# A decoder layer on one core: the causal mask moved from VectorE's scores to GpSimd's selects on the sigmoids, and two reorderings in the feed-forward part

## The chip, the cores and the metric

The kernel runs on one core of one Trainium2 chip. A core has a matrix engine (PE, with its weight loads PEld), VectorE (DVE), ScalarE (ACT), GpSimd (POOL) and a sync engine (SP) whose queue issues most DMAs. Each engine takes its instructions in order. The metric is the device time of one execution in microseconds; the time before is the median of three runs.

## The reference, cut to what matters

One decoder layer over 2048 tokens of width 1024: a norm, an input projection, two mixing groups (a causal convolution of width 31, and eight heads of causal stick-breaking attention), an output projection, a residual, and a SwiGLU feed-forward network of width 2816 with a residual. The part that the mask belongs to:

```python
z = einsum("bhqd,bhkd->bhqk", qb, kh) * scale
mask = key_pos[None, :] < q_pos[:, None]        # a token does not read itself
log_beta = log_sigmoid(z)
log_1m_beta = where(mask, log_sigmoid(-z), 0.0)
between = cumsum(log_1m_beta, axis=3, reverse=True) - log_1m_beta
attn = where(mask, exp(log_beta + between), 0.0)
```

So each weight is sigmoid(z) times the product of 1 - sigmoid(z) over the later keys. A masked key must give a factor of 1 in the product and a weight of 0.

## The kernel before, in words

**Tiling.** Tokens go in four groups of 512 (`g`), each of four 128-token tiles. Float32 products are made of three matmuls over split operands (H and L). A list `PLAN` names the stages on PE (input projection, output projection, first parts of the feed-forward network), and beside them run three "sides" with due positions: the attention, the convolution's taps (on DVE) and `sums`, which prepares combined feed-forward weights (on POOL).

**Order of instructions.** The text of the kernel gives each instruction a priority, in the order in which it is traced; the framework's scheduler then picks, engine by engine, what its model holds ready, higher priority first. So instructions traced late can run early. `tc.keep_in_program_order` pins an instruction behind the one traced just before it on the same engine. The feed-forward matmuls and the function `dve` (VectorE work of the loop `five`) are pinned so.

**Attention.** For each group, head (8) and key block `c` (from the diagonal one down to 0), `scores(u, j)` treats four tiles of 128 queries. Two matmuls write scores to a PSUM bank `z` (two of them, L563 and L564). On the diagonal block the width is (j + 1) x 128, and DVE adds `msk`, -1e30 above the diagonal, to the last 128 columns (L566). ACT makes `om` = sigmoid(-z/8) (L569) and `A` = sigmoid(z/8) (L571). DVE scans `om` from the right into running products (L573), which also reads `z`, so that the bank is free only after it, except in the last four heads of the last group. POOL multiplies `A` by the products (L574) and copies one column on for the next key block (L568, L576). `values` transposes `A` on PE (L590), splits it into TH (ACT, L248) and TL (DVE, L249), and multiplies by V (L595, L596). There are 128 diagonal calls of `scores` and 192 others.

**Feed-forward, gate and up.** It is done by a scheme with seven products of half size (numbered 1 to 7), whose right-hand sides are `B[g][n]`. `operands` loads such a side in four pieces (SP, L816), splits it on ACT (L810) and subtracts on DVE (L811). The loop `five` starts with block 0: `first` is product 6, and `second` adds a stored piece to it on DVE (L1061) before product 7 accumulates onto the same bank. Before the loop, sides 6, 5, 7 and 3 of the first half are loaded, 3 into tiles that the last output projection has just read. Product 3 of a block comes after products 7 and 5 and the next block's 6.

**Feed-forward, down.** 154 slots, each one pair of fetched pieces (SP loads, ACT splits L1279 and L1281, subtractions on POOL L1280 and DVE L1282, in rings of four) and 12 matmuls (L763). Slots go by product n = 1, 2, 6, 7, 4, 5, 3, eleven each, for two halves. When a row of the output is complete (n = 5, and n = 3), jobs are listed: `squares` (an ACT sum of squares, and a product by the gain on POOL, L1292) and `finish` (two POOL instructions that make the scale, L1297 and L1299, two DVE sums of 128x512, L1302, and the store of the row on SP, L1303). One job is traced to a slot. The last three slots are traced row by row, and their rows finished at once.

Of the kernel before, what the change touches and what calls it, by code (L numbers as in the profile page):

```python
# [9 lines left out]
F32 = mybir.dt.float32  # L10
# [3 lines left out]
ALU = mybir.AluOpType  # L14
# [4 lines left out]
P = 128  # L19
# [9 lines left out]
G = 512  # L29
NG = S // G  # L30
TT = G // P
# [3 lines left out]
NEG = -1e30  # L35
# [103 lines left out]
def layer_kernel(ctx: ExitStack, tc: tile.TileContext, x, xT, g_pre_mix, w_in, conv_w, conv_b, ln_g, ln_b,  # L139
                 attn_g, w_out, g_post_mix, g_pre_ffn, w_gate, w_up, w_down, g_post_ffn, out):  # L140
    nc = tc.nc
# [120 lines left out]
    def to_col(rows, k, Hs, Ls, g, banks=bank):  # L262

        ps = banks("tps")
        for t in range(TT):
# [24 lines left out]
    ident = ev("ident")[:, 0:P]  # L290
    make_identity(nc, ident)
    nc.vector.tensor_copy(idr, ident)
    msk = cc.tile([P, P], F32, name="msk")
    nc.gpsimd.memset(msk, NEG)
    nc.gpsimd.affine_select(msk, msk, pattern=[[1, P]], compare_op=ALU.is_ge, fill=0.0, base=0,
                            channel_multiplier=-1)
    one = cc.tile([P, 1], F32, name="one")
    nc.gpsimd.memset(one, 1.0)

# [234 lines left out]
    def attn(g):  # L534
# [20 lines left out]
        def scores(u, j):  # L555
            hd_ = heads[u["h"]]
            diag = u["c"] == g
            w = (j + 1) * P if diag else G
            K = u["K"]
            z = pp.tile([P, G], F32, tag="z", name="z")  # L560
            late = g == NG - 1 and u["h"] >= NH // 2
            js = slice(j * P, (j + 1) * P)
            nc.tensor.matmul(z[:, 0:w], hd_["QL"][:, js], K[:, 0:w], start=True, stop=False)  # L563
            nc.tensor.matmul(z[:, 0:w], hd_["QH"][:, js], K[:, 0:w], start=False, stop=True)  # L564
            if diag:
                nc.vector.tensor_tensor(z[:, w - P:w], z[:, w - P:w], msk, ALU.add)  # L566
            om = ap.tile([P, G + 1], F32, tag="om", name="om", bufs=NOM)
            nc.gpsimd.tensor_copy(om[:, G:G + 1], hd_["prev"][j])  # L568
            nc.scalar.activation(om[:, G - w:G], z[:, 0:w], AF.Sigmoid, scale=-0.125)  # L569
            a = ap.tile([P, G], F32, tag="A", name="A", bufs=NA)  # L570
            nc.scalar.activation(a[:, 0:w], z[:, 0:w], AF.Sigmoid, scale=0.125)  # L571
            r = om[:, G - w:G + 1][:, ::-1]
            nc.vector.tensor_tensor_scan(r, r, (one if late else z[:, 0:1]).to_broadcast([P, w + 1]), one, ALU.mult, ALU.bypass)  # L573
            nc.gpsimd.tensor_tensor(a[:, 0:w], a[:, 0:w], om[:, G - w + 1:G + 1], ALU.mult)  # L574
            pv = sp.tile([P, 1], F32, tag="pv", name="pv", bufs=8)
            nc.gpsimd.tensor_copy(pv, om[:, G - w:G - w + 1])  # L576
            hd_["prev"][j] = pv
            u["A"].append(a)
            return w
# [56 lines left out]
        for n in range(len(units) + 1):  # L636
            u = None
            if n < len(units):
                h, c = units[n]
# [345 lines left out]
    with ExitStack() as E:  # L985
# [113 lines left out]
        def five(early, todo):  # L1099


            NB = len(blocks)

            class Block:
                def __init__(self, n):
                    self.n = n
                    self.g, self.i, self.j = blocks[n]
                    self.A = {}
                    self.ahead = weights(*blocks[n], self.A)
                    next(self.ahead)  # L1110
                    self.s1 = next(s1_)
                    self.c11 = self.A["c11"]
                    nc.sync.dma_start(self.s1, stored["c11", self.g, self.i, self.j, 0])
                    nc.sync.dma_start(self.c11, stored["c11", self.g, self.i, self.j, 1])

                def mul(self, ps, n, start):
                    product(ps, n, self.A, B[self.g], start)
                    flush(2)

                def first(self):  # L1120
                    self.b2 = gu("b2")
                    self.mul(self.b2, 6, True)

                def second(self):
                    self.u2 = next(u_)
                    dve(self.u2, self.b2, self.s1, add)

                def split(self):
                    if "L" in self.A:
                        self.A["L"]()  # L1130

            b = Block(0)
            for _ in b.ahead:
                pass
            b.split()
            b.first()
            b.second()
            behind = []
            more_h = []
            for n in range(NB):  # L1140
                b3 = gu("b3")
                b.mul(b.b2, 7, False)
                nxt = Block(n + 1) if n + 1 < NB else None
                for fn, *args in behind:
                    fn(*args)
                c11 = result(b.i, (1, 1), b.c11)
                b.mul(b3, 5, True)
                u3 = next(u_)
                dve(u3, b.b2, b.s1, add)
                p4_ = b.A.get("p4")  # L1150
                if p4_ is not None:
                    dve(p4_, u3, p4_, add)
                if more_h:
                    next(more_h.pop())
                dve(u3, b3, u3, add)
                if nxt:
                    next(nxt.ahead)
                    nxt.first()
# [12 lines left out]
                if p4_ is None:  # L1171
                    p4_ = b.b2
                    dve(p4_, p4_, b.s1, add)
                c21 = result(b.i, (2, 1), p4_)
                b.mul(b3, 3, False)
                c21()
                dve(b3, b3, b.u2, add)
                behind = [(result(b.i, (1, 2), b3),)]
                if b.i:
                    more_h.append(hidden(b.g, b.j))  # L1180
                    behind.append((next, more_h[0]))
                behind += todo.get(n, ())
                b = nxt
            for fn, *args in behind:
                fn(*args)
            next(more_h.pop())
            assert next(more, None) is None
            next(more_wd)
            for _ in range(12):
                flush(2)  # L1190

        operands(0, [(6, x2), (5, x2), (7, e[4:6]), (3, e[0:2])])
        R = []
        last = NG - 2

# [95 lines left out]
            nc.scalar.activation(junk, t, AF.Square, scale=D ** -0.5, accum_out=ss[g][:, c, q:q + 1])  # L1291
            eng.tensor_tensor(t, t, gm[:, c * G:(c + 1) * G], mult)  # L1292

        def finish(T, r, cs):
            ms = sp.tile([P, 1], F32, tag="msf", name="msf", bufs=4)
            g, q = T // (2 * TT), T % (2 * TT)
            nc.gpsimd.tensor_scalar(ms, ss[g][:, 0, q:q + 1], ss[g][:, 1, q:q + 1], EPS, add, add)  # L1297
            rs = sp.tile([P, 1], F32, tag="rs", name="rs", bufs=4)
            nc.gpsimd.tensor_tensor(rs, ms, nhalf[:, 0:1], ALU.pow)  # L1299
            for (c, t) in enumerate(cs):  # L1300
                cs_ = slice(c * G, (c + 1) * G)
                nc.vector.scalar_tensor_tensor(r[:, cs_], t, rs, r[:, cs_], mult, add)  # L1302
            nc.sync.dma_start(out[T * P:(T + 1) * P, :], r)  # L1303

        LASTJ = 3
        slots = [(g, n, j) for g in (0, NG - 2) for n in (1, 2, 6, 7, 4, 5, 3) for j in range(HF)]
# [14 lines left out]
        for i, (g, n, j) in enumerate(slots):  # L1321
# [12 lines left out]
            if j == HF - 1:  # L1334
                for t, ps in enumerate(pss):
# [5 lines left out]
                    elif n in (6, 7):  # L1341
                        nc.vector.tensor_tensor((u2s if n == 6 else u3s)[t], ps, s1s[t], add)
                    elif n == 4:
                        nc.vector.tensor_tensor(s1s[t], ps, s1s[t], add)
                        jobs.append((squares, TB + t, 0, s1s[t]))
                    elif n == 5:
                        nc.vector.tensor_tensor(u3s[t], ps, u3s[t], add)
                        jobs.append((squares, TB + t, 1, u3s[t]))
                        jobs.append((finish, TB + t, hrows[t], (s1s[t], u3s[t])))
                    else:  # L1350
                        if ending:
                            for m in range(LASTJ):
                                slot(i - LASTJ + 1 + m, t, ps)
                        nc.vector.tensor_tensor(u2s[t], ps, u2s[t], add)
                        if ending:
                            squares(TA + t, 1, u2s[t], nc.vector)
                            finish(TA + t, hrows[TT + t], (c11s[t], u2s[t]))
                        else:
                            jobs.append((squares, TA + t, 1, u2s[t]))
                            jobs.append((finish, TA + t, hrows[TT + t], (c11s[t], u2s[t])))  # L1360
            elif jobs:
                fn, *args = jobs.pop(0)
                fn(*args)
        assert not jobs
    C.close()

# [56 lines left out]
```

## Time and profile before

| | us |
|---|---|
| median of 3 runs | 2562.7 (2555.69 to 2565.44) |
| profiled execution, its own time | 2551.76 |
| its span, first to last instruction | 2549.9 |

The mean granted clock of PE in the profiled execution is 0.983. The profile gives, for each engine, busy time; for each group of like instructions (line, engine, tiles, shapes), count, busy time, mean duration in ns, and the idle time of the engine just before them with what ended it. A wait's row reads: engine, tile and line that waited, what ended the wait, total us, times, longest. A timeline row reads: start, duration, engine, line, operation, tiles, count, and in brackets the engine's idle time before it and what ended that. Where a wait is for several things the profile names the one that came last by its records.

The stages in the trace: attention and projections up to about 1500 us, the loop `five` from about 1523 to about 2120 us, `down` from there to the end.

### The profile page before, as it was taken

How to read it: one execution, taken by the hardware profiler on the slowest of the kernel's cores; microseconds unless marked ns; L12 is line 12 of the kernel's file. 1: busy time of each engine (PE TensorE's matmuls, PEld its weight loads, DVE VectorE, ACT ScalarE, POOL GpSimd, SP SyncE). 2: the span in 40 equal slices, each digit the busy share in tenths (PEclk: the TensorE clock that was granted, in tenths of full speed). 3: DMA queues.
4: the chain of work that ended last, by engine and by line, in shares of the span. 5: the costliest groups of instructions: out<-in, count | busy, mean ns of one | idle time of the engine just before them, and what ended most of it. 6: DMA issues, size and time to landing. Idle time of an engine off the chain costs nothing. (4 is left out here: it accounts for less than half of the span.)

```text
span 2549.9 us, 35685 instructions
## 1 busy us (share of the span) xinstructions
PE 2422.0 (95%) x11156; PEld 1956.1 (77%) x11156; DVE 1806.7 (71%) x2321; ACT 1291.8 (51%) x2398; POOL 1518.6 (60%) x1844
## 2 busy tenths in 40 slices
PE   7999989998999999999999979999999999998997
PEld 6878767776777778887788857777788888886886
DVE  5797689977998797886655547667666664556556
ACT  4555555655655655667766644333322324454443
POOL 5764678555643666449634428755656564567556
PEclk9999989998999999999999989999999999999999
DMA  9989977987586698747877747977878768668665
GB/s 348 324 294 321 289 253 272 379 281 243 199 288 199 217 332 305 264 145 248 306 227 236 236 138 283 321 252 242 311 272 276 264 235 279 192 194 284 199 190 173
DMA packets 289181, 657.31 MB, mean 258 GB/s; under 512 B 33888, under 2 KB 42080, under 8 KB 288992
## 3 DMA queue, kind: packets, MB, share of 16 engines
q1 hardware_dynamic: 264704, 622.01, 72.7%
q10 hardware_dynamic: 24288, 33.04, 3.7%
q8 instruction: 88, 1.44, 0.2%
q14 instruction: 101, 0.83, 0.1%
HBM read 460.92 MB, written 193.99 MB: 257 GB/s over the span
## 5 line engine op out<-in xcount | busy, mean ns | idle before, releaser
L574 POOL TENSOR_TENSOR A<-A,om 128x512 f32<-128x512 f32 (+2 forms) x320 | 327.4, 1024 | 357.5 <-DVE om L573 234.9
L1054 POOL TENSOR_TENSOR wL<-raw,wH 128x512 fp32r<-128x512 f32 x176 | 253.5, 1463 | 202.7 <-ACT wH L1053 196.9
L476 DVE SCALAR_TENSOR_TENSOR cv<-glu,cw,cv 128x512 f32<-128x512 f32 x464 | 346.8, 748 | 6.7
L573 DVE TENSOR_TENSOR_SCAN om<-om,one,z 128x513 f32<-128x513 f32 (+3 forms) x256 | 278.0, 1098 | 62.4 <-ACT A L571 48.6
L1282 DVE TENSOR_TENSOR xL__21961<-t__21963,xH__21960 128x512 fp32r<-128x512 f32 x154 | 196.7, 1286 | 158.7 <-ACT xH__21960 L1281 158.7
L1280 POOL TENSOR_TENSOR xL__21959<-t__21962,xH__21958 128x512 fp32r<-128x512 f32 x154 | 209.7, 1367 | 165.5 <-ACT xH__21958 L1279 160.9
L256 PE MATMUL inps<-xH,wL 128*128 128x512 f32 x640 | 259.5, 406 | 5.5 <-ACT sg L422 5.5
L260 PE MATMUL inps<-xL,wH 128*128 128x512 f32 x640 | 257.2, 403 | 0.0
L258 PE MATMUL inps<-xH,wH 128*128 128x512 f32 x640 | 257.1, 402 | 0.0
L249 DVE TENSOR_TENSOR TL<-at,TH 128x512 fp32r<-128x512 f32 (+1 forms) x320 | 188.4, 598 | 89.1 <-ACT TH L248 88.5
L569 ACT ACTIVATE om<-z 128x512 f32<-128x512 f32 (+2 forms) x320 | 171.3, 538 | 157.8 <-DVE z L566 67.5
L763 PE MATMUL dps<-xH__21958,xL__21961 128*128 128x512 f32 x616 | 241.1, 391 | 10.3 <-DVE xL__21961 L1282 8.9
L763 PE MATMUL dps<-xL__21959,xH__21960 128*128 128x512 f32 x616 | 240.6, 391 | 3.2 <-POOL xL__21959 L1280 3.2
L763 PE MATMUL dps<-xH__21958,xH__21960 128*128 128x512 f32 x616 | 240.5, 390 | 0.0
L248 ACT ACTIVATE TH<-at 128x512 fp32r<-128x512 f32 (+1 forms) x320 | 168.6, 546 | 98.2 <-PE at L590 84.5
L1279 ACT ACTIVATE xH__21958<-t__21962 128x512 fp32r<-128x512 f32 x154 | 97.1, 631 | 229.0 <-POOL xL__21959 L1280 142.3
L590 PE MATMUL at<-idr,A 128*128 128x128 f32 x1088 | 191.2, 279 | 6.0 <-POOL A L574 3.8
L210 ACT ACTIVATE wH<-raw 128x1024 fp32r<-128x1024 f32 x156 | 165.8, 1063 | 55.1 <-DMA raw<-in_w_in_dram 23.0
L1053 ACT ACTIVATE wH<-raw 128x512 fp32r<-128x512 f32 x176 | 101.1, 623 | 158.9 <-PE b L763 65.1
L590 PEld LDWEIGHTS at<-idr,A 128*128 128x128 f32 x1088 | 142.0, 144 | 42.2 <-POOL A L574 6.1
L571 ACT ACTIVATE A<-z 128x512 f32<-128x512 f32 (+2 forms) x320 | 168.1, 540 | 10.8 <-PE at L590 10.5
L847 POOL TENSOR_TENSOR sum<-sum 128x512 f32<-128x512 f32 x88 | 115.6, 1313 | 74.6 <-DMA sum<-in_w_up_dram 42.4
(301 smaller groups left out, 6380.3 us busy)
## 6 DMA issues: line engine op xcount, KB each, us to landing
wL<-wL SPq DMA_DIRECT2D x156, 512.0 KB, 4.7
raw<-in_w_in_dram SPq DMA_DIRECT2D x80, 512.0 KB, 5.9
t__21963<-u SPq DMA_DIRECT2D x154, 256.0 KB, 2.8
c<-c ACTq DMA_DIRECT2D x88, 256.0 KB, 4.5
t__21962<-wd SPq DMA_DIRECT2D x88, 256.0 KB, 3.0
K<-kd SPq DMA_DIRECT2D x80, 256.0 KB, 4.4
V<-vd SPq DMA_DIRECT2D x80, 256.0 KB, 3.9
u<-accf SPq DMA_DIRECT2D x22, 768.0 KB, 4.3
```

The source lines that it names most:

```text
L249: nc.vector.tensor_tensor(L, ps, H.bitcast(F32), ALU.subtract)
L256: nc.tensor.matmul(ps, WL[:, kc], aH[t](k), start=k == 0, stop=False)
L258: nc.tensor.matmul(ps, WH[:, kc], aH[t](k), start=False, stop=False)
L260: nc.tensor.matmul(ps, WH[:, kc], aL[t](k), start=False, stop=k == KT - 1)
L476: nc.vector.scalar_tensor_tensor(to, gl[c][:, k:k + G], cw[:, c, k:k + 1], a, ALU.mult, ALU.add))
L573: nc.vector.tensor_tensor_scan(r, r, (one if late else z[:, 0:1]).to_broadcast([P, w + 1]), one, ALU.mult, ALU.bypass)
L574: nc.gpsimd.tensor_tensor(a[:, 0:w], a[:, 0:w], om[:, G - w + 1:G + 1], ALU.mult)
L590: nc.tensor.transpose(pt[:, j * P:(j + 1) * P], u["A"][j][:, b * P:(b + 1) * P], id32)
L763: return nc.tensor.matmul(ps, a, b, skip_group_check=True, **flags)
L1054: nc.gpsimd.tensor_tensor(l, t, f32(h), sub)
L1280: nc.gpsimd.tensor_tensor(WL, w, f32(WH), sub)
L1282: nc.vector.tensor_tensor(UL, t, f32(UH), sub)
```

## The change

1. The mask tile and the DVE addition go. After both sigmoids of a diagonal call, POOL runs an affine select on the last 128 columns of each: 1.0 into `om` and 0.0 into `A` where the key is not before the query.
2. Side 3 of the first half is no longer loaded with sides 6, 5 and 7 ahead of the loop, but is traced after `first` and `second` of block 0.
3. In `down`, `finish` does one half of a row; the scale is made at the first half and kept for the second; the store is a job of its own (`put`). A slot takes one job, or two if the first is a store; in the last slots as many as are needed to empty the list.

```diff
-    msk = cc.tile([P, P], F32, name="msk")
-    nc.gpsimd.memset(msk, NEG)
-    nc.gpsimd.affine_select(msk, msk, pattern=[[1, P]], compare_op=ALU.is_ge, fill=0.0, base=0,
-                            channel_multiplier=-1)
...
-            if diag:
-                nc.vector.tensor_tensor(z[:, w - P:w], z[:, w - P:w], msk, ALU.add)
             om = ap.tile([P, G + 1], F32, tag="om", name="om", bufs=NOM)
             nc.gpsimd.tensor_copy(om[:, G:G + 1], hd_["prev"][j])
             nc.scalar.activation(om[:, G - w:G], z[:, 0:w], AF.Sigmoid, scale=-0.125)
             a = ap.tile([P, G], F32, tag="A", name="A", bufs=NA)
             nc.scalar.activation(a[:, 0:w], z[:, 0:w], AF.Sigmoid, scale=0.125)
+            if diag:
+                for t, x, fill in ((om, G, 1.0), (a, w, 0.0)):
+                    t = t[:, x - P:x]
+                    nc.gpsimd.affine_select(t, t, pattern=[[-1, P]], compare_op=ALU.is_ge, fill=fill, base=-1,
+                                            channel_multiplier=1)
...
             b.first()
             b.second()
+            operands(0, [(3, e[0:2])])
...
-        operands(0, [(6, x2), (5, x2), (7, e[4:6]), (3, e[0:2])])
+        operands(0, [(6, x2), (5, x2), (7, e[4:6])])
...
-        def finish(T, r, cs):
+        def scale_of(T, c):
+            if c:
+                return scales.pop(T)
             ms = sp.tile([P, 1], F32, tag="msf", name="msf", bufs=4)
             g, q = T // (2 * TT), T % (2 * TT)
             nc.gpsimd.tensor_scalar(ms, ss[g][:, 0, q:q + 1], ss[g][:, 1, q:q + 1], EPS, add, add)
             rs = sp.tile([P, 1], F32, tag="rs", name="rs", bufs=4)
             nc.gpsimd.tensor_tensor(rs, ms, nhalf[:, 0:1], ALU.pow)
-            for (c, t) in enumerate(cs):
-                cs_ = slice(c * G, (c + 1) * G)
-                nc.vector.scalar_tensor_tensor(r[:, cs_], t, rs, r[:, cs_], mult, add)
+            scales[T] = rs
+            return rs
+
+        def finish(T, r, t, c):
+            rs = scale_of(T, c)
+            cs_ = slice(c * G, (c + 1) * G)
+            nc.vector.scalar_tensor_tensor(r[:, cs_], t, rs, r[:, cs_], mult, add)
+
+        def put(T, r):
             nc.sync.dma_start(out[T * P:(T + 1) * P, :], r)
+
+        def rest(T, r, cs):
+            return [(finish, T, r, t, c) for c, t in enumerate(cs)] + [(put, T, r)]
...
-                        jobs.append((finish, TB + t, hrows[t], (s1s[t], u3s[t])))
+                        jobs += rest(TB + t, hrows[t], (s1s[t], u3s[t]))
...
             elif jobs:
-                fn, *args = jobs.pop(0)
-                fn(*args)
+                left = len(slots) - i - LASTJ
+                for _ in range(-(-len(jobs) // max(left, 1)) if left < HF else 2 if jobs[0][0] is put else 1):
+                    if jobs:
+                        fn, *args = jobs.pop(0)
+                        fn(*args)
```

More of the change, by code (lines that the diff above doesn't have):

```diff
@@ L1299, in finish @@
             nc.gpsimd.tensor_tensor(rs, ms, nhalf[:, 0:1], ALU.pow)
[L1300 to L1302 removed]
+            scales[T] = rs
+            return rs
+        scales = {}
+        def finish(T, r, t, c):
[3 more added lines that the diff above has]
+        def put(T, r):
             nc.sync.dma_start(out[T * P:(T + 1) * P, :], r)
+        def rest(T, r, cs):
+            return [(finish, T, r, t, c) for c, t in enumerate(cs)] + [(put, T, r)]
         LASTJ = 3
@@ L1356, in layer_kernel @@
                             squares(TA + t, 1, u2s[t], nc.vector)
-                            finish(TA + t, hrows[TT + t], (c11s[t], u2s[t]))
+                            for fn, *args in rest(TA + t, hrows[TT + t], (c11s[t], u2s[t])):
+                                fn(*args)
                         else:
                             jobs.append((squares, TA + t, 1, u2s[t]))
-                            jobs.append((finish, TA + t, hrows[TT + t], (c11s[t], u2s[t])))
+                            jobs += rest(TA + t, hrows[TT + t], (c11s[t], u2s[t]))
             elif jobs:
-                fn, *args = jobs.pop(0)
-                fn(*args)
+                left = len(slots) - i - LASTJ
+                for _ in range(-(-len(jobs) // max(left, 1)) if left < HF else 2 if jobs[0][0] is put else 1):
+                    if jobs:
+                        fn, *args = jobs.pop(0)
+                        fn(*args)
         assert not jobs
```

## The prediction

> **What bounds the kernel now.** I read the first part of the page, then the waits of TensorE (PE) by stage, then the timeline at each long one.
>
> ```profile
> span 2549.9 us, 35685 instructions
> PE 2422.0 (95%) x11156; PEld 1956.1 (77%) x11156; DVE 1806.7 (71%) x2321; ACT 1291.8 (51%) x2398; POOL 1518.6 (60%) x1844
> ...
> PE 27%; POOL 2%; DVE 2%; DMA 2%; issue 1%; ACT 0%; SPq 0%; POOLq 0%; DVEq 0%; ACTq 0%
> ```
>
> PE is busy 2422.0 of 2549.9 us and leads the chain that ended last. The change takes no matmul away, so what it can win is PE's idle time, 127.9 us (5%), and time in which PE runs at half pace behind a pause. I therefore price each edit by the PE waits that it touches. The mask lies in the attention stage, 64 to 1430 us:
>
> ```profile
> 64.00:1430.00 1366.00, 1302.87 (x6334) 1052.64 (x6333) 1071.07 (x1537) 818.88 (x1552) 806.03 (x1275) 0.98 0.80 267
> ...
> PE z L563 <- DVE om L573: 23.3, 31, 2.7
> PE o L596 <- DVE TL L249: 10.8, 16, 1.7
> ```
>
> The first row holds the busy time of PE, PEld, DVE, ACT, POOL in that window; the others are waits (us, times, longest). PE idles 1366 - 1302.87 = 63.1 us there, 23.3 of it for a score bank that the scan (DVE L573) has not let go. DVE is busy 78%, POOL 59%.
>
> **The change, part by part: the mask.** Removed from DVE: 128 additions. Added to POOL: 256 affine selects of 128x128, an instruction that this trace shows in its prologue.
>
> ```profile
> L566 DVE TENSOR_TENSOR z<-z,msk 128x128 f32<-128x128 f32 x128 | 36.7, 291 | 38.4 <-PE z L564 38.2
> ACT om L569 <- DVE z L566: 67.5, 41, 6.4
> 1.62 0.29 POOL L295 TENSOR_SCALAR_AFFINE_SELECT msk<-msk 128x128 f32<-128x128 f32 x1
> L563 PE MATMUL z<-K,QL 128*128 128x512 f32 x224 | 97.2, 434 | 15.3 <-DVE om L573 14.4 <-DMA vd<-vt 0.7
> ```
>
> - DVE loses 128 x 0.291 = 36.7 us of work, and 38.2 us in which it stood at an addition waiting for scores. ACT no longer waits 67.5 us (41 times) for the addition: 0.5 us for each of 128 diagonal units.
> - POOL gains 256 x 0.29 = 74.2 us, 5% of the stage: 59% becomes 64%. The memset and select of the mask (0.2 + 0.29 us) go from the prologue, where the engines wait for input DMAs: nothing.
> - Sigmoid, scan and product keep shapes and counts. But the scan, in DVE's in-order queue, now waits for the select of om, which stands in POOL's in-order queue behind whatever is there. Behind the scan are the taps and the TL subtractions, for which PE waits. The select of A sits before the product on the same engine: 0.29 us of POOL's idle time.
>
> On one side the gain is at most what the narrow diagonal scores wait for (the 512-wide ones wait 14.4 of 23.3 us, so the others 8.9) and the 10.8 us for TL: 19.7. On the other stands what a late select costs; the nearest rows are those in which POOL's head holds up a scan today:
>
> ```profile
> 605.89 1.26 POOL L847 TENSOR_TENSOR sum<-sum 128x512 f32<-128x512 f32 x1 [5.72 <-DMA sum<-in_w_up_dram]
> 607.31 1.28 DVE L573 TENSOR_TENSOR_SCAN om<-om,one,z 128x513 f32<-128x513 f32 x1 [3.44 <-POOL om L568]
> 608.65 0.50 PE L563 MATMUL z<-K,QL 128*128 128x512 f32 x1 [2.68 <-DVE om L573]
> POOL sum L847 <- DMA sum<-in_w_up_dram: 42.4, 12, 10.4
> POOL sum L847 <- DMA sum<-in_w_gate_dram: 20.0, 11, 7.9
> POOL wL L214 <- ACT wH L210: 31.4, 12, 4.9
> ```
>
> A sum waits 5.72 us for its DMA, the one-column copy behind it is late, the scan stalls 3.44 us and PE 2.68. Such foreign waits at POOL's head make 42.4 + 20.0 + 31.4 = 93.8 us, 7% of the stage. If 7% of 128 selects (9) meet one of 2.7 us (93.8 / 35), scans wait 24 us, PE 2.68/3.44 of it, 19 us. Mostly a select lands between products of 1.0 to 1.2 us, which costs as much as the 0.5 us saved. I take 7 us gained: the 8.9 us of the narrow banks largely, a little of TL, less a few late selects. Ends: 19.7 gained, 19 lost.
>
> The Trainium skill ("GPSIMD Engine Reference", section 4.1 Engine selection) would keep elementwise work on VectorE: GpSimd is about twice slower with two inputs and about line rate with one. The row bears out the exception, 0.29 us against VectorE's 0.291. Priced as two-input work at twice that, POOL would gain 149 us by estimate, and the late-select rival would weigh more.
>
> **P3's side.** Moving operand 3 behind `second` moves four loads on SP, four ACT splits and four DVE subtractions. `second` is pinned behind the DVE instruction traced before it: today the last of those subtractions.
>
> ```profile
> 1499.49 2.12 SPq L816 DMA_DIRECT2D sumin<-B  x4
> 1525.71 0.40 PE L763 MATMUL b<-xL__17306,wH 128*128 128x512 f32 x1
> 1524.87 4.66 DVE L811 TENSOR_TENSOR e__17360<-sumin,e__17359 128x512 fp32r<-128x512 f32 x4 [0.83 <-ACT e__17359 L810]
> 1529.45 0.68 DVE L1061 TENSOR_TENSOR glu<-b,glu 128x512 f32<-128x512 f32 x1
> 1530.28 0.47 PE L763 MATMUL b<-e__17341,wL 128*128 128x512 f32 x1 [4.17 <-POOL ms L191]
> 1531.38 0.63 PE L763 MATMUL b<-e__17341,wL 128*128 128x512 f32 x1
> 1531.81 0.63 PE L763 MATMUL b<-e__17341,wH 128*128 128x512 f32 x1
> 1534.23 0.39 PE L763 MATMUL b<-e__17341,wH 128*128 128x512 f32 x1
> 1534.46 0.39 PE L763 MATMUL b<-e__17342,wH 128*128 128x512 f32 x1
> ```
>
> The product ends at 1526.1; `second` (glu) runs only at 1529.45, behind the four subtractions of 1.165 us; PE restarts after 4.17 us. (The row names POOL's ms; glu ends 0.15 us before PE starts, and it is glu that must read the bank before PE adds to it.) Then eight matmuls run 0.43 us apart instead of 0.23: 8 x 0.2 = 1.6 us more. With `second` free of the pin, it waits for one running subtraction at most: 1526.1 + 1.17 + 0.68 + 0.15 = 1528.1, a wait of 2.0 instead of 4.17. Elsewhere PE paused 2.4 us and the next matmul took full pace (below, 2307.37), so the 1.6 go too: 3.8 us. Ends: nothing, if all four subtractions still run first as they are ready earlier; 4.17 - 0.8 + 1.6 = 5.0 if none does. The subtractions end some 0.7 us later; P3's product comes three products of 2.8 us (12 x 0.23) behind, which covers it. The four loads, issued on SP at 1499.49, come to stand behind the first block's weight loads; they have the 25 us up to the subtractions in hand. A later wait could give some back: 3 us taken.
>
> The Trainium skill ("TensorE: Matmul & The Clock Gate", Part 1) puts the array at half clock after an idle window of about 3.4 us. By it a wait left at 3.5 us would keep the slow 1.6 us, and the edit would be worth 0.7; the 4.17 and 2.37 us rows agree with it.
>
> **The row ends.** Work is the same; `finish` becomes two halves and a store, each a job of its own.
>
> ```profile
> 2292.30 1.15 POOL L1297 TENSOR_SCALAR msf<-ss 128x1 f32<-128x1 f32 x1
> 2293.53 1.30 POOL L1292 TENSOR_TENSOR e__21967<-e__21967,gain 128x512 f32<-128x512 f32 x1
> 2302.17 1.78 DVE L1302 SCALAR_TENSOR_TENSOR e__21969<-t__21965,rs,e__21969 128x512 f32<-128x512 f32 x1
> 2303.87 1.77 DVE L1302 SCALAR_TENSOR_TENSOR e__21969<-e__21967,rs,e__21969 128x512 f32<-128x512 f32 x1
> 2305.57 4.65 DVE L1282 TENSOR_TENSOR xL__21961<-t__21963,xH__21960 128x512 fp32r<-128x512 f32 x4
> 2296.95 0.50 PE L763 MATMUL dps<-xL__21959,xH__21960 128*128 128x512 f32 x1 [0.61 <-POOL xL__21959 L1280]
> 2307.37 0.50 PE L763 MATMUL dps<-xH__21958,xL__21961 128*128 128x512 f32 x1 [2.37 <-DVE xL__21961 L1282]
> 2333.50 0.50 PE L763 MATMUL dps<-xL__21959,xH__21960 128*128 128x512 f32 x1 [2.00 <-POOL xL__21959 L1280]
> 2343.92 0.50 PE L763 MATMUL dps<-xH__21958,xL__21961 128*128 128x512 f32 x1 [2.41 <-DVE xL__21961 L1282]
> 2518.49 0.50 PE L763 MATMUL dps<-xL__21959,xH__21960 128*128 128x512 f32 x1 [0.61 <-POOL xL__21959 L1280]
> 2528.89 0.50 PE L763 MATMUL dps<-xH__21958,xL__21961 128*128 128x512 f32 x1 [2.38 <-DVE xL__21961 L1282]
> ```
>
> At three row ends DVE runs final sums in a heap, up to 1.78 us each, and the operand subtractions (L1282) behind them keep PE waiting: 0.61 + 2.37, 2.00 + 2.41, 0.61 + 2.38, in all 10.4 us. Split jobs rank behind more operand work, so sums and subtractions should alternate. Against it: jobs stand one to a slot of 2.8 us (12 matmuls) already, yet row ends came in a burst; one row's msf (2292.30) and the next row's product by the gain (2293.53) stand 1.2 us apart, where their slots are two apart: the scheduler pulls ready work forward whatever its slot. At the last row end both versions use two slots a row. I take half of the first two, 7.4 us: 4, and nothing of the last. Ends: 7.4 gained; 3 lost, if a late store on SP holds a load behind it by a slot.
>
> **Sum.** 7 + 3 + 4 = 14 us. The profiled execution took 2551.76 us (span 2549.9): 2538 on its footing. It lies 10.9 us under the median of the runs, 2562.7; on that footing 2548.
>
> **Rivals.** Half a per cent, 12.8 us, is about what a measurement here tells from no change.
>
> - Likeliest: the sum, 2548; its own range 2536 to 2558.
> - Reordering eats it. The scheduler floats selects, splits and row ends to where they are ready; `second` still runs behind the subtractions, the row ends still heap, and the mask trades one queue for another at 0.5 us each. Left: about 4 us, 2559. For it: the burst above. Against: the pin on `second` does go.
> - Slower: selects stuck at POOL's head. 9 late selects lose 19 us of PE; each pause above 3 us adds half-paced matmuls, 1.6 us a time. With one select in eight late, 16 x 2.7 x 0.78 = 34 us, against 12 us still won (3 + 4, and 5 of the mask's): 22 lost, 2585. It decides from about 12 late ones (25 - 12 = 13 us). For it: the 605.89 row. Against: POOL has 41% idle, and its copies today cost scans only 6.3 us in sum:
>
> ```profile
> DVE om L573 <- POOL om L568: 6.3, 4, 3.4
> ```
>
> - More gain: with 75 us off DVE's queue (36.7 + 38.2), all 19.7 us of scan and TL waits, 5 and 7.4 go: 32 us, 2531.
>
> **Chances.** The sum 0.38, reordering 0.32, slower 0.16, more gain 0.14. Of the sum's outcomes some fall short of 12.8 us, so faster takes most of 0.38, and 0.14: 0.47; same 0.36; slower 0.17. The range 2524 to 2578 goes from just past the full gain to short of the stuck selects.
>
> **What would show it.** Mask: L566 gone, 256 selects near 0.29 us, "z waits for om" under 23.3 us; wrong if a wait of the scan for POOL's select appears above some 25 us. P3: glu starts before the last L811 subtraction and the 4.17 us pause is at or under 2; wrong if it stays. Row ends: waits for L1282 and L1280 at the first two under 4 us; wrong if final sums still stand in a row of six. The whole is wrong if PE's idle time does not fall, or the order of the attention stage changes for other reasons and moves it by more than 15 us.

## The result and the profile after

The changed kernel takes 2571.5 us (median), before takes 2555.9 in the same session: ratio 1.0055, 95% interval 1.004 to 1.007. It is 16 us slower where I forecast 14 us faster. Two executions of it were profiled, 2580.3 us (called "after" below) and 2573.1 ("second profile"); the second is near the median, so the stage readings are from it. Executions of one program spread over 10 to 14 us, so all verdicts below go by ratios over the runs with their 95% intervals, and a row of a trace is only read for its mechanism.

The head of after's page: PE's span share falls by a point, DVE loses 10 us (23 in the second profile), POOL gains 72.

```profile
span 2578.6 us, 35988 instructions
PE 2431.4 (94%) x11156; PEld 1962.4 (76%) x11156; DVE 1796.2 (70%) x2193; ACT 1292.6 (50%) x2398; POOL 1590.5 (62%) x2098
```

The attention stage, from 64 us to the first matmul of the last gate-and-up stage, by windows: before, then the second profile.

```profile
64.00:1523.00 1459.00, 1384.23 (x6693) 1116.57 (x6692) 1118.90 (x1597) 867.62 (x1639) 835.08 (x1316) 0.98 0.78 261
```

```profile
64.00:1542.00 1478.00, 1389.55 (x6704) 1119.26 (x6703) 1094.21 (x1469) 868.60 (x1640) 908.30 (x1573) 0.97 0.77 259
```

The stage is 19 us longer. PE idles 1478 - 1389.55 = 88.5 us in it instead of 74.8; the other 5.3 us are busy time, for 11 matmuls more (some 2 us) and at a granted clock of 0.97 instead of 0.98. The rest of the kernel is 2.5 us longer (2571.4 - 1542 against 2549.9 - 1523). So the loss lies in the stage of the mask; the first experiment shows that it is the mask's.

The selects, and the waits of the second profile (64 to 1560 us):

```profile
L570 POOL TENSOR_SCALAR_AFFINE_SELECT A<-A 128x128 f32<-128x128 f32 x128 | 40.6, 321 | 30.5 <-ACT A L565 29.6 <-DVE om L573 0.2
L570 POOL TENSOR_SCALAR_AFFINE_SELECT om<-om 128x128 f32<-128x128 f32 x128 | 40.6, 318 | 69.6 <-ACT om L563 64.2 <-PE z L560 3.8 <-DMA kd<-qkL 1.2
```

```profile
ACT om L563 <- PE z L560: 131.8, 99, 6.6
POOL om L570 <- ACT om L563: 64.2, 43, 4.2
DVE om L573 <- POOL om L570: 34.5, 26, 4.2
PE z L559 <- DVE om L573: 27.4, 31, 3.3
```

Before, ACT waited for the scores so long, beside the 67.5 us for the addition:

```profile
ACT om L569 <- PE z L564: 63.9, 50, 6.3
```

A select takes 0.32 us instead of the 0.29 priced: 81 us for 256. The scan (L573) waits 34.5 us, 26 times, for a select; before it waited 6.3 us for POOL's one-column copy and 13.1 us for POOL in all. POOL in turn stands idle ahead of selects for 100 us (69.6 + 30.5), nearly all of it until ACT has made the sigmoid. PE's wait for a score bank did not fall: 27.4 against 23.3. And ACT gained nothing by the addition's going: it waits 131.8 us for the scores now, where it waited 63.9 + 67.5 = 131.4 us for the scores and the addition.

**One place that shows it.** Around 135 us PE stops for 5.2 to 6.3 us in each profile of the changed kernel itself (four orders, below) and in no profile of before. Second profile, ACT and PE:

```profile
133.90 1.06 ACT L210 ACTIVATE wH<-raw 128x1024 fp32r<-128x1024 f32 x1 [4.33 <-DMA raw<-in_w_in_dram]
135.13 0.27 ACT L563 ACTIVATE om<-z 128x128 f32<-128x128 f32 x1
135.28 0.28 ACT L565 ACTIVATE A<-z 128x128 f32<-128x128 f32 x1
136.44 0.65 ACT L660 ACTIVATE oT<-o 128x512 f32<-128x512 f32 x1
137.14 0.80 PE L595 MATMUL o<-TH,V 128*128 128x512 f32 x1 [5.88 <-ACT oT L660]
```

The same place before:

```profile
130.59 1.06 ACT L210 ACTIVATE wH<-raw 128x1024 fp32r<-128x1024 f32 x1 [5.41 <-DMA raw<-in_w_in_dram]
131.55 0.58 ACT L660 ACTIVATE oT<-o 128x512 f32<-128x512 f32 x1
132.18 0.50 PE L595 MATMUL o<-TH,V 128*128 128x512 f32 x1 [1.13 <-ACT oT L660]
```

In both, ACT's queue stands behind a weight that a DMA brings. Before, the copy of `oT`, which frees PE's bank `o`, is next; in the changed kernel it comes after the sigmoids of two diagonal units, and the weight lands 3.3 us later. Nothing here is a late select: it is the other order that the scheduler draws once the work of a diagonal unit looks different to it. Why the weight landed later was not traced. Nor is this stop the whole loss: e6 and e11 below have selects and lose as much or more, and wait only 0.9 and 1.7 us for `oT` there.

**P3's side and the row ends, after.** DVE and PE at the first, DVE and PE at the second:

```profile
1554.29 4.06 DVE L811 TENSOR_TENSOR e__17775<-sumin,e__17774 128x512 fp32r<-128x512 f32 x3 [0.84 <-ACT e__17774 L810]
1558.27 0.68 DVE L1061 TENSOR_TENSOR glu<-b,glu 128x512 f32<-128x512 f32 x1
1559.09 0.47 PE L763 MATMUL b<-e__17722,wL 128*128 128x512 f32 x1 [3.57 <-POOL rs L192]
...
2329.50 0.74 DVE L1312 SCALAR_TENSOR_TENSOR e__22349<-e__22348,rs,e__22349 128x512 f32<-128x512 f32 x1
2330.82 1.78 DVE L1312 SCALAR_TENSOR_TENSOR e__22350<-e__22348,rs,e__22350 128x512 f32<-128x512 f32 x1
2335.93 4.64 DVE L1283 TENSOR_TENSOR xL__22342<-t__22344,xH__22341 128x512 fp32r<-128x512 f32 x4
2337.73 0.50 PE L763 MATMUL dps<-xH__22339,xL__22342 128*128 128x512 f32 x1 [2.44 <-DVE xL__22342 L1283]
2373.46 0.50 PE L763 MATMUL dps<-xH__22339,xL__22342 128*128 128x512 f32 x1 [2.41 <-DVE xL__22342 L1283]
```

Three of the four subtractions still run ahead of `second` (glu); the pause is 3.57 us instead of 4.17. The final sums (L1312) still stand six in a row (2327.80 to 2336.0, two of them shown), the subtractions behind them, and PE's waits are 2.44 and 2.41 where they were 2.37 and 2.41.

### The profile page after: what moved, and what is told of

The parts are those of the page before. It is cut to its first block, busy times and chain, and to the rows that moved or that the text cites. A ratio compares the mean times of both kernels' runs of the same rounds, so it can differ in the third digit from the quotient of the medians.

```text
span 2578.6 us, 35988 instructions
## 1 busy us (share of the span) xinstructions
PE 2431.4 (94%) x11156; PEld 1962.4 (76%) x11156; DVE 1796.2 (70%) x2193; ACT 1292.6 (50%) x2398; POOL 1590.5 (62%) x2098
## 5 line engine op out<-in xcount | busy, mean ns | idle before, releaser
L574 POOL TENSOR_TENSOR A<-A,om 128x512 f32<-128x512 f32 (+2 forms) x320 | 319.3, 999 | 251.6 <-DVE om L573 185.5
L573 DVE TENSOR_TENSOR_SCAN om<-om,one,z 128x513 f32<-128x513 f32 (+3 forms) x256 | 276.4, 1097 | 67.6 <-ACT A L565 45.0
```

## The experiments

"Before" and "after" are the two kernels, with the attention's due times ending at 870 (`ATTN = ((46, 0.0), (870, 1.0))`). Ratios are to before, from the same chip and session.

**The two other edits alone (e1).**

```diff
 # after, with before's mask back
+nc.vector.tensor_tensor(z[:, w - P:w], z[:, w - P:w], msk, ALU.add)
-nc.gpsimd.affine_select(t, t, ...)      # on om and on A
```

> The kernel before with P3's side fetched later and the row ends split, and the mask still added by VectorE. In the changed kernel's trace three of the four subtractions still run ahead of `second` (the pause is 3.57 us instead of 4.17) and the six final sums still stand in a row at each row end. Theory 'these two edits do nothing': within 3 us of before. Rival 'they cost part of the loss': 4 us slower or more. Rival 'they gain as forecast and the mask loses all the more': 4 to 8 us faster.

Measured 2556.6 us, ratio 1.0001 (0.9991 to 1.0011). Within 3 us they do nothing, as the rows above suggest, and the scores stand where they stood in TensorE's order (0 matmuls later); the loss comes with the mask.

**Is it the selects, or another order of the same work?** The scheduler's order changes with any edit: counted in TensorE's instruction order, after issues the attention's scores 42 projection matmuls later than before, on average. Left out altogether, the mask changes the order about as much (39). The due time shifts the order and nothing else.

```diff
 # e2: before without the addition of the mask (left out: the output lacks it; the two other edits are not in)
 # e3: before, e4: after, each with another end of the due times
-ATTN = ((46, 0.0), (870, 1.0))
+ATTN = ((46, 0.0), (880, 1.0))     # e3; e4 has 860
```

> The kernel before without the mask's addition and with no select in its place: the mask is left out altogether (128 VectorE additions, 36.7 us, gone; GpSimd gets nothing). In the built program PE's order puts the attention on average 39 matmuls of other work later than before, about as in the changed kernel (42). Theory 'late selects': without selects nothing can be late, so 5 to 15 us faster than before. Theory 'order': the loss is that the scheduler draws the attention later and leaves its end uncovered, which this kernel does as well; 8 to 15 us slower than before though it has less work.

> The kernel before with one number changed, the due position at which the attention ends (870 to 880), which puts the attention on average 40 matmuls later in PE's order, as the changed kernel does; the mask stays on VectorE. Theory 'late selects': no difference beyond 5 us. Theory 'order': 8 to 15 us slower.

> The changed kernel with the attention's end due at 860 instead of 870: PE's order then has the attention on average 7 matmuls earlier than before, and the selects stay on GpSimd. Theory 'late selects': still 10 to 16 us slower than before. Theory 'order': within 5 us of before, or faster.

Measured: e2 0.9984 (0.9971 to 0.9996), e3 1.007 (1.0051 to 1.0088), e4 1.0096 (1.0078 to 1.0114). They contradict each other if lateness or late selects alone are the cause: e3 loses as much as after with no select in it, but e2 is as late as after and loses nothing, and e4, whose scores come no later than before's (-7), loses more than after. So both kernels had to be measured over several orders.

> Before, with the end of the attention's due times at 850 instead of 870 (nothing else; its score units come 41 matmuls earlier in TensorE's order). If the loss of 16 us is only that the change draws another order, orders of before spread as widely as those of after: this one lies anywhere in 2545 to 2575, and the mean of before's four orders (850, 860, 870, 880) is that of after's four within 5 us. If the selects cost time in any order: 2550 to 2562, and before's mean is 12 to 20 us under after's.

> Before at 860; its units come 41 matmuls later, as those of after and of e3. If lateness in the order costs the time: as e3, 2570 to 2576. If the selects do: 2552 to 2565, and e3 was one unlucky order.

> The changed kernel at 850; its units come 16 matmuls later than before's. If lateness costs the time: 2560 to 2566, between before and after. If the selects cost in any order: 2568 to 2582.

> The changed kernel at 880; its units come 88 matmuls later than before's. If lateness costs the time: twice the loss of after, 2585 to 2595. If the selects cost and lateness little: 2568 to 2582 again.

> e2 (mask left out altogether, both other edits in) with the due times' end at 860. Before's four orders have the ratios 1.002, 0.999, 1 and 1.007, after's 1.0092, 1.0096, 1.0055 and 1.012. If the mask on VectorE costs what the prediction's 19.7 us bound says and e2 drew an unlucky order: 0.990 to 0.995. If the mask on VectorE is nearly hidden: 0.996 to 1.004, and no place for it can win more than a few us.

> The same at 880. Hidden mask: 0.996 to 1.006; mask worth 19.7 us: 0.990 to 0.996.

Where the expectation for e17 says "both other edits in", the kernel is, like e2, before without the mask. Ratios with their intervals (lateness in matmuls in brackets):

| due times end at | before | after | mask left out |
|---|---|---|---|
| 850 | 1.002, 1.0006 to 1.0035 (-41) | 1.0092, 1.0066 to 1.0119 (16) | |
| 860 | 0.999, 0.9977 to 1.0004 (41) | 1.0096, 1.0078 to 1.0114 (-7) | 0.9991, 0.9977 to 1.0004 (23) |
| 870 | 1 | 1.0055, 1.004 to 1.007 (42) | 0.9984, 0.9971 to 0.9996 (39) |
| 880 | 1.007, 1.0051 to 1.0088 (40) | 1.012, 1.0086 to 1.0154 (88) | 1.0009, 0.9994 to 1.0024 (43) |

Lateness does not explain it: 40 and 41 later give 1.007 and 0.999. An order by itself moves the time by 0.8%. Beyond that, the means over orders are 1.002 for before and 1.0091 for after: the selects cost 0.7%, 18 us. The size is rough, since four orders each that scatter by 0.8 and 0.65%, and overlap (before's 1.007, after's 1.0055), leave some 0.2 to 1.3% open, by an estimate from their scatter. Over the three orders that all have, before has 1.002, after 1.009, no mask 0.9995: on GpSimd the mask costs 0.95%, 24 us. On VectorE it costs 0.25%, 6 us, in the mean, but 0, 4 and 16 us in the single orders, so that this is not told from nothing.

Already in the first 276 us the groups separate. By windows, before, no mask (e2), and after (second profile):

```profile
64.00:340.00 276.00, 266.13 (x1307) 217.02 (x1306) 209.35 (x344) 148.50 (x298) 172.62 (x265) 0.98 0.91 302
```

```profile
64.00:340.00 276.00, 261.22 (x1307) 213.91 (x1305) 200.88 (x296) 150.06 (x300) 170.29 (x263) 0.99 0.89 297
```

```profile
64.00:340.00 276.00, 260.44 (x1276) 214.13 (x1275) 188.09 (x277) 142.26 (x282) 192.08 (x341) 0.97 0.91 304
```

The matmuls done by then are 1307 in before and without mask, 1276 with selects; the other orders give 1298, 1312 and 1312 for before, 1311 and 1313 without mask, and 1274, 1272 and 1267 for after (1244 in the first profile at 870). The difference of the means over four orders is 35. 35 matmuls at 266.13 / 1307 = 0.2 us are 7 us by estimate, more than a third of the loss.

PE's waits in the attention stage also separate, when they are summed by the engine that ended them. Those that VectorE ended are 50.5 to 62.4 us in before's four orders and 51.8 to 60.1 in after's (means 56.3 and 56.5). Those that ScalarE ended are 12.2 to 16.8 us in before's, 12.7 to 13.7 without mask, and 18.4 to 26.7 in after's (means 14.4, 13.1 and 22.9); 5.2 to 5.9 of after's are the stop at 135 us. So scans wait for selects, but the pauses that PE has more stand behind ScalarE, not behind the scans' engine.

**Who waits for the select (e5, e6).** Same 256 selects, all on the tile that only GpSimd's own product reads, or all on the tile that the scan needs. The expectations say "as after", but the rest of both kernels is before without the addition; the two other edits, worth nothing by e1, are not in them.

```diff
 # before without the addition; behind the two sigmoids of a diagonal call (shortened):
+for t, x, fill in ((a, w, 0.0),):        # e6: ((om, G, 1.0),)
+    select(t[:, x - P:x], fill); select(t[:, x - P:x], fill)
```

> As after, but both selects of a unit fall on A, which only GpSimd's own product reads; om keeps its unmasked diagonal block (that part of the mask is left out). GpSimd has the same 256 selects, no scan waits for one. If the loss lies in scans that wait for a select, this stands near the kernel without mask, 2553 to 2561. If it lies in the 81 us that GpSimd has more to do, whoever waits, it stands near after, 2568 to 2580. The row of scans that wait for L570 is gone either way.

> The mirror: both selects on om, for which the scan waits; A's diagonal block is unmasked (that part is left out). 256 selects again. If scans that wait for a select cost the time: at or above after, 2571 to 2590, and the scan's wait for L570 above the 33 us of after. If it is GpSimd's load: the same as e5.

Measured: e5 1.0072 (1.005 to 1.0093), e6 1.0157 (1.0134 to 1.018). Waits, 64 to 1430 us, e5 and then e6:

```profile
POOL A L571 <- ACT A L565: 85.3, 30, 10.0
```

```profile
DVE om L574 <- POOL om L571: 52.4, 28, 4.8
PE o L597 <- DVE TL L249: 16.9, 16, 4.1
```

With 52.4 us of scans that wait for a select, e6 takes 22 us more than e5, which has none. Here the late scans do reach PE: it waits 16.9 us for the TL subtractions, which stand behind the scans in VectorE's queue (10.8 in before, 5.8 in e5), and its waits that VectorE ended are 87.0 us in the stage, against 57.5 in e5. But e5 loses 18 us with no such scan. There the selects hold up only GpSimd's own queue, 85.3 us at ACT's second sigmoid, and ScalarE ended 22.7 us of PE's waits, as in after. Both expectations were half right. Each is one order (62 and 54 matmuls later), and an order alone moved before by 0.8%, so neither 18 nor 22 us is the price of the waits alone.

**Is it GpSimd's load, or its long runs beside VectorE (e9, e10, e11)?** In the profile of after, one subtraction on DVE took 12.54 us.

```profile
406.77 1.29 POOL L361 TENSOR_TENSOR xcol<-xcol,rb 128x512 f32<-128x512 f32 x1
408.84 3.79 POOL L361 TENSOR_TENSOR xcol<-xcol,rb 128x512 f32<-128x512 f32 x3
408.85 12.54 DVE L388 SCALAR_TENSOR_TENSOR xL<-xcol,gpm,xH 128x512 fp32r<-128x512 f32 x1 [0.22 <-ACT xH L387]
413.64 4.92 POOL L361 TENSOR_TENSOR xcol<-xcol,rb 128x512 f32<-128x512 f32 x4
420.77 0.65 POOL L576 COPY pv<-om 128x1 f32<-128x1 f32 x1
422.69 0.80 PE L689 MATMUL ops<-wH,xL 128*128 128x512 f32 x1 [10.32 <-DVE big L694]
```

GpSimd runs two-input instructions without a gap; the subtraction, 0.75 us elsewhere, ends only when GpSimd comes to a one-column copy; PE loses 10.32 us. e9 is after once more; e10 splits the multiplications; e11 moves them to VectorE.

```diff
-nc.gpsimd.tensor_tensor(r[:, i, :], r[:, i, :], rbs[g], mult)
+for c in range(0, G, P):                                   # e10
+    nc.gpsimd.tensor_tensor(r[:, i, c:c + P], r[:, i, c:c + P], rbs[g][:, c:c + P], mult)
+nc.vector.tensor_tensor(r[:, i, :], r[:, i, :], rbs[g], mult)   # e11, in its place
```

> The changed kernel once more, for a second profile. If the 12.54 us that one xL subtraction (L388, 0.74 us elsewhere) took at 408.85 us belongs to this program, it is there again within a few us, at the same place, with PE's wait of some 10 us behind it, and the span lies near 2570 to 2578. If it was a mishap of one execution, all 24 of L388 lie under 3 us and the span is 8 to 12 us shorter, 2565 to 2570.

> The changed kernel with each of GpSimd's 24 multiplications of xcol in four of 128x128 (TensorE's order stays nearly the same). If VectorE is held off by GpSimd's unbroken run of two-input instructions and gets in at an instruction's end, L388 falls under 3 us and some 8 to 10 us come back: 2560 to 2564. If an instruction's end does not let it in, L388 stays at 7 to 13 us and the time is that of after, or 1 to 3 us more for GpSimd's 96 shorter instructions: 2571 to 2575.

> The changed kernel with the 24 multiplications of xcol on VectorE, so that GpSimd has no such run beside the subtraction, and 31 us less in all (VectorE 16 us more). If GpSimd's load and its long runs are what the selects ran into: L388 under 2 us and 2556 to 2562. If the selects cost by their order and their waits alone: 2568 to 2576, and only the one long L388 is gone.

Measured: e9 2573.1 us in one execution, the same instruction there 1.84 us; e10 1.0116 (1.0093 to 1.014); e11 1.0074 (1.0049 to 1.0099).

```profile
403.39 1.84 DVE L388 SCALAR_TENSOR_TENSOR xL<-xcol,gpm,xH 128x512 fp32r<-128x512 f32 x1 [0.22 <-ACT xH L387]
```

So the 12.54 us was a mishap of that execution (e5 and e6 had such ones too, 9.12 and 7.36 us) and not the loss. In e10 the longest still took 4.9 us, across eight ends of GpSimd's instructions, up to a one-column copy: an instruction's end does not let VectorE in. e10 also gave GpSimd 10 us more (24 multiplications of 1.3 us became 96 of 0.43), and lost 16 us against after in nearly its order (43 matmuls later), more than I expected. e11 takes 31 us off GpSimd, long runs included, gives VectorE 21, and stands at 1.0074, among after's four orders (1.0055 to 1.012). So nothing is seen to come back; but it draws another order (20 matmuls later), and e10 points the other way, so GpSimd's load is not ruled out.

**What the other two edits would be worth if the order were held (e7, e8, e12).** All three are e1 with pins: `tc.keep_in_program_order` on the four subtractions of P3's side (e7); besides, on the operand subtractions, gains, scales, bank sums and final sums of down (e8); on those of the first group's row ends alone, and not on P3's side or the bank sums (e12).

```diff
-nc.vector.tensor_tensor(UL, t, f32(UH), sub)
+keep(nc.vector.tensor_tensor(UL, t, f32(UH), sub))
 # the same for WL, the gain, msf, rs and the final sum; in e12 keep() pins only in these slots:
+keeping[:] = [1] * ((g, n) in ((0, 5), (0, 3), (NG - 2, 1)))
```

> e1 (mask on VectorE, the two other edits) with the four subtractions of P3's side held to the traced order, behind the first result of the last stage. If the edit failed only since they were free to run first: the pause of 4.17 us before the second product falls to 2 or less, the half pace behind it goes, and the time falls by 3 to 5 us, to 2552 to 2554. If the pause has another cause, 2556 to 2557 and the pause stays.

> e7, and in down the subtractions, gains, scales, bank sums and final sums of VectorE and GpSimd held to the traced order, so that final sums and operand subtractions alternate. If the heap costs what its waits show (0.61 + 2.37 and 2.00 + 2.41 at the first two row ends, 0.61 + 2.38 at the last): 5 to 10 us under e7, 2543 to 2549. If an order held by hand makes subtractions wait for bank sums or scales: slower than e7 by a few us, with new waits for L1282's and L1280's tiles at every product's end.

> e1 (mask on VectorE, both other edits) with only the first group's row ends held to the traced order: operand subtractions, gains, scales and final sums alternate, from the fifth product's slots to the end of the next group's first product; P3's side and the last row end are left as in e1. In e8 TensorE did not pause at these row ends, but paused where the pins stood elsewhere (4.84 at the start of down, six times 0.43, 2.15 at the end). If that is all: the waits of e1 there (0.55 + 2.42, 1.48, 0.76) and of before (0.61 + 2.37, 2.00 + 2.41, 1.44) go, and the time is 5 to 9 us under before, 2548 to 2553. If the alternation shifts the waits: within 2 us of e1.

e7: 1.0008 (0.9995 to 1.0021), no gain, though the pause did go:

```profile
1530.72 0.69 DVE L1064 TENSOR_TENSOR glu<-b,glu 128x512 f32<-128x512 f32 x1 [2.08 <-PE b L763]
1531.33 3.08 DVE L809 TENSOR_TENSOR e__17394<-sumin,e__17393 128x512 fp32r<-128x512 f32 x4
1531.56 0.47 PE L763 MATMUL b<-e__17341,wL 128*128 128x512 f32 x1 [0.88 <-DVE glu L1064]
1537.15 2.30 DVE L723 SCALAR_TENSOR_TENSOR big<-big,rs,gain 128x1024 f32<-128x1024 f32 x1
1541.25 0.69 DVE L1064 TENSOR_TENSOR cy<-b,cy 128x512 f32<-128x512 f32 x1
1542.09 0.61 PE L763 MATMUL b<-e__17393,wL 128*128 128x512 f32 x1 [1.92 <-DVE cy L1064]
1570.95 0.80 PE L763 MATMUL b<-e__17393,wL 128*128 128x512 f32 x1 [4.09 <-DVE cs L1064]
```

PE waits 0.88 us where it waited 4.17. Then 1.92 two products on, at half pace again, and 4.09 at 1570.95, around which e1's longest pause is 0.95: the last layer's residual work (L723, up to 2.3 us) shares DVE's queue through this stretch, and what is not late now is late then. The pauses over 0.3 us from 1520 to 1640 us add up to 10.8 us in e1 and in e7.

e8: 1.0029 (1.0016 to 1.0042), slower. PE:

```profile
2115.36 0.79 PE L763 MATMUL dps<-xH__21958,xL__21961 128*128 128x512 f32 x1 [4.84 <-DVE xL__21961 L1286]
2300.44 0.47 PE L763 MATMUL dps<-xH__21958,xL__21961 128*128 128x512 f32 x1 [0.43 <-DVE e__21967 L1366]
2421.18 0.47 PE L763 MATMUL dps<-xH__21958,xL__21961 128*128 128x512 f32 x1 [0.43 <-DVE e__21966 L1361]
2539.66 0.80 PE L763 MATMUL dps<-xH__21958,xL__21961 128*128 128x512 f32 x1 [2.15 <-DVE xL__21961 L1286]
```

From 2300.44 to 2421.18, over both row ends of the first group, the timeline shows no pause of PE. What it lost stands elsewhere: pinned, the first subtractions queue behind the last sums of the stage before (4.84), and subtractions behind bank sums (0.43, six times). e12 keeps only the good part: **2546.4 us, ratio 0.9954 (0.9937 to 0.9972)**, the one version here with the whole mask that is faster than before. DVE, and then down by windows, e12 and e1:

```profile
2321.43 1.78 DVE L1318 SCALAR_TENSOR_TENSOR e__21969<-t__21965,rs,e__21969 128x512 f32<-128x512 f32 x1 [0.77 <-POOL rs L1309]
2323.12 1.78 DVE L1289 TENSOR_TENSOR xL__21961<-t__21963,xH__21960 128x512 fp32r<-128x512 f32 x1
2324.83 1.77 DVE L1318 SCALAR_TENSOR_TENSOR e__21969<-e__21967,rs,e__21969 128x512 f32<-128x512 f32 x1
```

```profile
2106.40:2542.00 435.60, 420.35 (x1849) 346.34 (x1848) 269.57 (x236) 202.20 (x381) 271.94 (x210) 0.99 0.66 222
```

```profile
2106.10:2550.60 444.50, 423.36 (x1849) 347.04 (x1847) 263.99 (x236) 201.81 (x380) 267.96 (x210) 0.99 0.65 217
```

Final sums and subtractions alternate, and down is 8.9 us shorter: 5.9 us of it are PE's idle time, 3.0 us its busy time, since matmuls at half pace behind the pauses went too. The last row end was not pinned (a wait of 2.42 us stays there), nor were pins tried without the split of `finish`.

## Why the prediction was wrong, point by point

- **The mask, 7 us gained: this step failed.** It cost 16 us, and 18 in the mean over four orders. The relief was small: the kernels without mask gain 0, 4 and 16 us in three orders, and ACT's 67.5 us at the addition became a longer wait for the scores, so that the "0.5 us saved" of a diagonal unit did not come. Above all the price of the selects failed. I counted 9 late ones, 24 us of scans, as the bad end and took it that most would cost nothing; the second profile has 26 waits that add up to 34.5 us, the other orders have 33.0 (850), 58.5 (860) and 47.5 (880), where before's four have 1.7 to 6.3 for the one-column copy. My own mark for "wrong", 25 us, was passed each time. I counted only what stands at POOL's head today and not the selects themselves, which stand there 100 us waiting for ACT.
- **How a late scan reaches PE** was wrong too. I passed on 0.78 of it to PE's wait for score banks; that wait is 20.7 to 27.4 us over after's four orders, 20.7 to 26.4 over before's, and all of PE's waits that VectorE ended stay at 56 us in the mean. PE waits 8.5 us more for ScalarE instead, for the most part at 135 us. That the selects cost the time is shown; by what path the rest of it reaches PE stays open. The order of the stage changed too, which I had named as a sign that the whole is wrong.
- **P3's side, 3 us gained: nothing.** Its 1.6 us for half pace rested on a short reading: behind the pause at 2307.37 only six matmuls keep full pace, then eight do not (last section), so that this row does not agree with an idle window of 3.4 us, as I wrote it does. The unpinned subtractions, "ready earlier", ran first: the lower end that I had named. And e7 shows that even the upper end was not there to win, since the same DVE queue stops PE at 1542 and 1571 us instead.
- **Row ends, 4 us gained: nothing.** That jobs emitted apart would run apart was the error, against the burst that I had quoted as evidence. The size was too small: held apart at the first two row ends, with the split in, they are worth 10 to 12 us (e12), more than the 7.4 that I set as the end, for I priced the waits alone and not the half pace behind them.
- **The rivals.** "Slower" named the selects, as the runs do, and was too dear, 2585, as it took one select in eight for late at 2.7 us; they are one in five (26 of 128) at 1.3 us, the 12 us set against them never came, and its path over the score banks was not the one. "Reordering eats it" was right for both small edits.
- By the rule in the Trainium skill ("GPSIMD Engine Reference", section 4.1 Engine selection) elementwise work belongs on VectorE. Its reason, the duration, does not apply here: 0.32 us against 0.29. Its advice held all the same, for another reason.
- A slip in the working: 128 x 0.291 is 37.2 us; the row's 36.7 us is its busy time as it stands. And 2571.5 us lies inside the range of 2524 to 2578 by the range's width alone, not by its reasons.

**Not settled:** what makes up e5's 18 us, what GpSimd's load has to do with it, and how much of after's loss is waits at queues and how much the order that the scheduler draws because of the selects. A kernel with before's order frozen and selects in it would tell; it was not tried.

## What to carry to other kernels

Moving work to an engine with 40% idle time is not free when the moved step stands between two others: price the wait at the head of the new queue in both directions (for its input, and by its reader), not only the busy time. When a scheduler reorders everything after an edit, compare several orders of both versions (here one number in a due time moved the time by 0.8%) before crediting the edit. An edit that is meant to change an order must bind it, and only where the profile shows the burst: pins gave 10 us at the first two row ends (e12), and a wider set, bank sums included, lost 5 over all of down (e8 against e7).

## What the hardware showed that I had not expected

- TensorE's half pace does not follow the length of the pause. In before, matmuls go on at full pace (0.23 us apart) after 2.41 us (2343.92) and 2.38 us (2528.89). After 2.37 us (2307.37) six keep full pace, and then eight come 0.40 to 0.43 us apart (two of them below). In after the same row end, 2.44 us (2337.73), has such a run too. After 1.92 us in e7 (1542.09) and 2.15 us in e8 (2539.66; 1.32 us three matmuls earlier) the next matmuls are 0.43 us apart, for 3.4 and 5.3 us. That a pause of 2.4 us keeps full pace was no rule. The Trainium skill ("TensorE: Matmul & The Clock Gate", Part 1) names an idle window of about 3.4 us that runs freely of the program. That the same pause can end either way fits a free-running window; that 1.92 us suffices doesn't fit an idle one of 3.4.

```profile
2309.26 0.63 PE L763 MATMUL dps<-xH__21958,xH__21960 128*128 128x512 f32 x1
2309.69 0.63 PE L763 MATMUL dps<-xL__21959,xH__21960 128*128 128x512 f32 x1
```

- VectorE can be held off by GpSimd for as long as GpSimd runs two-input instructions without a gap: 12.54, 9.12 and 7.36 us for a subtraction of 0.75, in the profiles of after, e5 and e6, and 4.90 in e10, each time up to a one-column copy; the same subtraction took 1.84 us in the second profile of after. The Trainium skill ("GPSIMD Engine Reference", section 1, Specifications) has GpSimd share VectorE's memory interfaces when VectorE reads two inputs from SBUF; the subtraction does, and in the second profile VectorE's other instructions beside that run keep their durations (0.68 to 0.80 us).
